# A fused two-layer decoder step: layer-norm statistics, squares and values to be split move from SBUF to PSUM

## The chip, the cores and the metric

The kernel runs on one core of one Trainium2 chip. Its time is the device time of one execution in microseconds (us), the median of several. Engines: PE is the matmul engine, DVE is VectorE, ACT is ScalarE, POOL is GpSimd, and SP issues most DMAs. Each has a queue of its own and works it off in order; semaphores hold an instruction until what it reads is written and the buffer that it writes is free. SBUF is the large on-chip memory. PSUM is the small one that PE writes its sums to: here eight banks of 512 numbers per partition, four with the tag `mm` and four with `tr`.

## The reference

Two layers run over 512 prompt tokens and 8 x 8 sample tokens with the same weights (576 columns in all). Each norm closes a residual step, and the values that follow feed the next projection:

```
h    = x * (1 + scale1) + shift1
proj = h @ w_in            # retention, sliding-window attention -> mix
x    = LN1(alpha * x + gate1 * (mix @ w_out))
h2   = x * (1 + scale2) + shift2
u    = causal depthwise conv3(h2 @ w_up);  f = (silu(u_a) * u_b) @ w_down
x    = LN2(alpha * x + gate2 * f)

mu  = mean(x);  var = mean((x - mu)^2)
LN  = (x - mu) * rsqrt(var + eps) * g + b
```

Outputs are the last `x` and the states of both groups.

## The kernel before

**Layout.** Features lie on partitions, tokens in columns: `X[0..7]` are eight tiles of 128 x 576. Work goes in two halves of 288 columns (`HA`); the second half holds 224 prompt columns and the 64 of the samples, whose gate, scale and shift differ per group of 8. That is why the second half needs small extra operations of 64 columns (L558, L560).

**Matmuls.** Products need nearly full float32. Each value is split into a rounded high part (`hi`, a cast on ACT, L290) and a rest (`lo`, a subtraction, L291), each weight likewise (`wh`, a cast on ACT, L91, and `wl`, a subtraction on POOL or DVE, L96). Every product is three matmuls: hi with wh, lo with wh, hi with wl (`gemm`). A projection of one half is 8 x 3 = 24 matmuls of 128x288. `Weights` loads weights in units of 128x1024 through two buffers `wr` (SP's queue); a load waits until the subtraction of the unit before last is done.

**The norm.** There are four: l0a and l0b after attention and after the feed-forward of layer 0, l1a and l1b in layer 1. `LayerNorm.r_done` runs as each tile `X[m]` of a half is ready: its square (ACT, L527) is added to `sq` (DVE, L528), the value to `sd` (POOL, or DVE for the last tile, L525). `stats` sums both over the partitions with a matmul by ones (`pd`, `pq`, in `tr` banks), squares the mean, subtracts it (L540), takes the root (ACT, L541) and the reciprocal (DVE, L542), and copies the mean to SBUF (ACT, L543). `norm` subtracts the mean (L548) and multiplies by the inverse (L549) for each k; `make_h` then forms `h` = x*scale + shift (ACT, L285), `hi` and `lo`.

**The order around it.** `halves` runs the last four output projections for half 0, then one for half 1, then statistics and norm of half 0, then the other three for half 1. `skewed` runs the next stage's first projections for half 0, with statistics and norm of half 1 after the first of them in the text, then for half 1. Each engine's order there is not written out: a scheduler of the compiler makes it from dependencies and free buffers, so a change of buffers moves instructions. The attention in between is pinned in written order.

**Names.** `l0a0...` is norm l0a, half 0, `l0a1...` half 1. `l0a1s` are squares, `l0asq` and `l0asd` the sums, `l0a0pd` and `l0a0pq` the PSUM results, `l0ars` the inverse. `l0wo` is the output projection, `l0up0h` the first up-projection of a half, `l0up4a` the first one after the skewed stage, `l0ghi` and `l0glo` the split values, `h0g` (l0b: `h0n`) the value before its split. `l1kv0h` is the first projection that follows l0b.

Of the kernel before, what the change touches and what calls it, by code (L numbers as in the profile page):

```python
# [121 lines left out]
def _body(ctx, tc, nc, a):  # L122
# [156 lines left out]
    def make_h(src, st, k, half, hi, lo, nm):  # L279

        s_t, t_t = st
        tmp = tok(f"h{nm}", HA)
# [1165 lines left out]
```

## Time and profile before

| | |
|---|---|
| median of 3 runs | 1529.6 us (1527.59 to 1530.27) |
| profiled execution | 1529.95 us, its span 1528.2 us |
| mean granted PE clock | 0.983 |
| PE busy | 1461.7 us, 96% of the span |
| DVE busy | 864.4 us, 57% |
| ACT busy | 643.0 us, 42% |
| POOL busy | 496.4 us, 32% |

A busy share is an average over the span: it says which engine is nearly always at work, not what is late in one stage. For that there are the list of waits (who was idle, and whose instruction ended the idle time), the timeline of an engine (each instruction with its start and duration), and the windows (busy time and granted clock in a stretch). [...] A timeline row with x2 or x3 is so many instructions in sequence.

### The profile page before, as it was taken

The numbers are of one execution on the slowest core, as the hardware profiler recorded it, in microseconds if no ns is written. First come the engines' busy times: TensorE is split into PE (matmuls) and PEld (weight loads), VectorE is DVE, ScalarE is ACT, GpSimd is POOL, SyncE is SP. The second block draws the span as 40 slices with busy tenths as digits, with TensorE's granted clock in tenths as the row PEclk, the third lists the DMA queues.
The fourth block names the chain that finished last, engine by engine and source line by source line (L and its number), as shares of the span: only waits on it lengthen the run. The fifth ranks groups of instructions, "written<-read, shape, count | busy, mean of one in ns | idle before, by whom it ended". The sixth has DMA issues, their size and how long they took to land.

```text
span 1528.2 us, 28103 instructions
## 1 busy us (share of the span) xinstructions
PE 1461.7 (96%) x11220; PEld 1368.5 (90%) x11220; DVE 864.4 (57%) x1659; ACT 643.0 (42%) x1295; POOL 496.4 (32%) x646
## 2 busy tenths in 40 slices
PE   6999989989999999999999999999799999999995
PEld 3878789979989998999988899889799999999994
DVE  3366356776644254545675664677775435544567
ACT  2335233347542144325446443333675325524543
POOL 2131212454421132223462322225543213312353
PEclk8999999999999999999999999999999999999998
DMA  9585733333364655332213333242132222223211
GB/s 347 162 284 171 244 117 105 103 104 92 101 228 157 228 167 179 93 106 83 80 56 130 118 112 97 85 113 66 56 102 85 85 84 85 83 80 93 84 49 63
DMA packets 98047, 186.37 MB, mean 122 GB/s; under 512 B 30284, under 2 KB 42620, under 8 KB 97788
## 3 DMA queue, kind: packets, MB, share of 16 engines
q1 hardware_dynamic: 82624, 176.52, 36.7%
q10 hardware_dynamic: 15292, 8.06, 1.8%
q8 instruction: 88, 1.44, 0.4%
q14 instruction: 43, 0.35, 0.1%
HBM read 169.56 MB, written 11.83 MB: 119 GB/s over the span
## 4 chain that ended last, share of the span: by engine, by line
PE 81%; DVE 11%; DMA 3%; ACT 2%; issue 1%; POOL 1%; SPq 0%; ACTq 0%; POOLq 0%; DVEq 0%
PE ada L135 3%; PE l0wo L135 1%; PE l1wo L135 1%; DVE l1x L548 1%; PE l0wdl L135 1%; PE l1wdl L135 1%; DMA wr<-in_wst 1%; DVE l0x L548 1%; DVE l1x L549 1%; DVE l0x L549 1%; DVE wl L96 1%; ACT l1p L663 1%; PE l1o L135 1%; PE l0o L135 1%; ACT wh L91 1%
## 5 line engine op out<-in xcount | busy, mean ns | idle before, releaser
L91 ACT CAST wh<-wr 128x1024 fp32r<-128x1024 f32 x192 | 200.5, 1047 | 316.1 <-PE l0rv2b L135 11.9
L96 POOL TENSOR_TENSOR wl<-wr,wh 128x1024 fp32r<-128x1024 f32 x65 | 158.1, 2432 | 399.1 <-ACT wh L91 349.2
L96 DVE TENSOR_TENSOR wl<-wr,wh 128x1024 fp32r<-128x1024 f32 x127 | 161.2, 1270 | 165.0 <-ACT wh L91 146.1
L1160 POOL COPY l0edge<-l0u 128x2 f32<-128x2 f32 x44 | 38.3, 871 | 134.1 <-ACT l0u L1154 134.1
L1160 POOL COPY l1edge<-l1u 128x2 f32<-128x2 f32 x44 | 38.3, 871 | 120.6 <-ACT l1u L1154 120.6
L1168 DVE SCALAR_TENSOR_TENSOR l0c<-l0u,par,l0c 128x592 f32<-128x592 f32 x44 | 48.3, 1100 | 49.3 <-ACT l0c L1167 46.7
L1168 DVE SCALAR_TENSOR_TENSOR l1c<-l1u,par,l1c 128x592 f32<-128x592 f32 x44 | 48.6, 1106 | 46.3 <-ACT l1c L1167 43.6
L135 PE MATMUL ada<-wa,cs 128*32 128x512 f32 (+1 forms) x416 | 59.2, 584 | 5.2 <-DVE cs L185 5.1
L135 PEld LDWEIGHTS ada<-wa,cs 128*32 128x32 f32 x416 | 15.0, 112 | 32.5 <-issue 17.5
L1167 ACT ACTIVATE l0c<-l0u,par 128x592 f32<-128x592 f32 x44 | 38.8, 884 | 3.6 <-ACT l0u L1155 0.4
L1167 ACT ACTIVATE l1c<-l1u,par 128x592 f32<-128x592 f32 x44 | 38.8, 884 | 3.3
L1169 DVE SCALAR_TENSOR_TENSOR l1c<-l1u,par,l1c 128x592 f32<-128x592 f32 x44 | 36.6, 834 | 1.4
L1169 DVE SCALAR_TENSOR_TENSOR l0c<-l0u,par,l0c 128x592 f32<-128x592 f32 x44 | 36.6, 834 | 1.4
L479 ACT CAST l0fhi<-l0c 128x512 fp32r<-128x512 f32 (+1 forms) x44 | 16.8, 430 | 46.5 <-DVE l0c L1174 46.5
L479 ACT CAST l1fhi<-l1c 128x512 fp32r<-128x512 f32 (+1 forms) x44 | 16.9, 431 | 37.8 <-DVE l1c L1174 37.8
L792 POOL TENSOR_TENSOR l1sw<-l1sw,c_sin 128x576 f32<-128x576 f32 x8 | 14.9, 1857 | 50.6 <-DMA l1sw<-l1raw 47.9
L792 POOL TENSOR_TENSOR l0sw<-l0sw,c_sin 128x576 f32<-128x576 f32 x8 | 13.6, 1697 | 43.9 <-DMA l0sw<-l0raw 43.9
L480 DVE TENSOR_TENSOR l1flo<-l1c,l1fhi 128x512 fp32r<-128x512 f32 (+1 forms) x44 | 18.2, 455 | 13.0 <-ACT l1fhi L479 13.0
L480 DVE TENSOR_TENSOR l0flo<-l0c,l0fhi 128x512 fp32r<-128x512 f32 (+1 forms) x44 | 18.2, 455 | 12.4 <-ACT l0fhi L479 12.4
L1173 ACT ACTIVATE l1c<-l1c 128x592 f32<-128x592 f32 x22 | 15.4, 698 | 15.2 <-DVE l1c L1169 15.2
L235 DVE TENSOR_TENSOR mod<-adat,par 128x36 f32<-128x36 f32 (+1 forms) x26 | 3.7, 185 | 31.6 <-PE adat L138 31.6
L1173 ACT ACTIVATE l0c<-l0c 128x592 f32<-128x592 f32 x22 | 15.3, 698 | 13.6 <-DVE l0c L1169 13.6
(3182 smaller groups left out, 5936.0 us busy)
## 6 DMA issues: line engine op xcount, KB each, us to landing
wr<-in_wst SPq DMA_DIRECT2D x192, 512.0 KB, 3.6
wa<-in_w_ada SPq DMA_DIRECT2D x192, 256.0 KB, 4.9
x<-in_xT SPq DMA_DIRECT2D x8, 288.0 KB, 6.2
l0sw<-l0raw SPq DMA_DIRECT2D x32, 72.0 KB, 2.0
l0xb<-in_xT SPq DMA_DIRECT2D x8, 288.0 KB, 3.3
x_spill<-l0x ACTq DMA_DIRECT2D x8, 288.0 KB, 3.2
l1sw<-l1raw SPq DMA_DIRECT2D x32, 72.0 KB, 2.1
l1xb<-x_spill SPq DMA_DIRECT2D x8, 288.0 KB, 3.1
```

The costliest lines, as they stand in the source:

```text
L91: cast = nc.scalar.copy(hi, raw)
L96: sub = eng.tensor_tensor(lo, raw, hi.bitcast(F32), ALU.subtract)
L135: self._add(nc.tensor.matmul(*args, **kw))
L479: S.copy(hi, src)
L480: V.tensor_tensor(lo, src, hi.bitcast(F32), ALU.subtract)
L548: eng.tensor_tensor(x[:, o], x[:, o], self.sd[:, o], ALU.subtract)
L549: (eng if both else V).tensor_tensor(x[:, o], x[:, o], self.rs[:, o], ALU.mult)
L1160: G.tensor_copy(cm[:, 0:2], t[:, 512:514])
L1167: S.activation(c, t[:, 0:592], AF.Identity, bias=w[3], scale=w[0])
L1168: V.scalar_tensor_tensor(c, t[:, 1:593], w[1], c, ALU.mult, ALU.add)
L1169: V.scalar_tensor_tensor(c, t[:, 2:594], w[2], c, ALU.mult, ALU.add)
L1173: S.activation(ca, ca, AF.Silu)
```

## The change

Six edits go together. `SKEW_TAGS` gives all skewed projections `mm` banks; before, every third one took a `tr` bank. The square `t` goes to a `tr` bank, and becomes the first operand of the add. In the three norms that are not the last, the reciprocal overwrites the bank `pq`, and the mean is read from the bank `pd`, without its copy. All subtractions of the mean and all `lo` are DVE's (before, `SUB_POOL` and `LO_POOL` gave POOL two or three subtractions and two `lo` of each half). The value `h` before its split lies in a `tr` bank. The last norm (`tail`) keeps its inverse and mean in SBUF and its share for POOL.

```
--- before.py
+++ after.py
@@ -30,12 +30,10 @@
 N_IN, N_OUT, N_UP, N_DN = 22, 8, 44, 22
 UNITS = N_IN + N_OUT + N_UP + N_DN
 MM = 4
-SKEW_TAGS = ("mm", "mm", "tr")
+SKEW_TAGS = ("mm",)
 SKEW_OUT = 4
 SKEW_DN = 4
 SKEW_END = 4
-SUB_POOL = ((6, 7), (5, 6, 7))
-LO_POOL = ((1, 3), (1, 3))
 Y_POOL = ((2, 4, 6), (2, 4, 6))
 Y_DVE = ((1, 5), (5, 7))
 HEADS = (slice(0, 64), slice(64, 128))
@@ -279,7 +277,7 @@
     def make_h(src, st, k, half, hi, lo, nm):
 
         s_t, t_t = st
-        tmp = tok(f"h{nm}", HA)
+        tmp = psum("tr", f"h{nm}")
         o = half * HA
         n = HA if half == 0 else NP - HA
         S.activation(tmp[:, 0:n], src[:, o:o + n], AF.Identity, bias=t_t[:, k, 0:1], scale=s_t[:, k, 0:1])
@@ -288,7 +286,7 @@
             V.tensor_tensor(tv, src[:, NP:NT].rearrange("p (b t) -> p b t", b=8), bc(s_t[:, k, 1:9], 2, 8), ALU.mult)
             V.tensor_tensor(tv, tv, bc(t_t[:, k, 1:9], 2, 8), ALU.add)
         S.copy(hi[:, o:o + HA], tmp[:, 0:HA])
-        (G if k in LO_POOL[half] else V).tensor_tensor(lo[:, o:o + HA], tmp[:, 0:HA], hi[:, o:o + HA].bitcast(F32), ALU.subtract)
+        V.tensor_tensor(lo[:, o:o + HA], tmp[:, 0:HA], hi[:, o:o + HA].bitcast(F32), ALU.subtract)
 
     scr = dp.tile([P, 8, 384], F32, name="bias_rows", tag="bias_rows")
     scr1 = dp.tile([8, 384], F32, name="bias_row", tag="bias_row")
@@ -487,12 +485,13 @@
     junk = cp.tile([P, 1], F32, name="junk", tag="junk")
 
     class LayerNorm:
-        def __init__(self, X, nm):
-            self.X, self.nm = X, nm
+        def __init__(self, X, nm, tail=False):
+
+            self.X, self.nm, self.tail, self.mean, self.inv = X, nm, tail, {}, {}
             self.shift = unit("S", f"{nm}sh")
             self.sd = unit("S", f"{nm}sd")
             self.sq = unit("S", f"{nm}sq")
-            self.rs = unit("S", f"{nm}rs")
+            self.rs = unit("S", f"{nm}rs") if tail else None
 
         def shift_base(self, m, half, base):
 
@@ -523,9 +522,9 @@
                 G.tensor_tensor(self.sd[:, o], self.X[0][:, o], x[:, o], ALU.add)
             else:
                 (V if m == 7 else G).tensor_tensor(self.sd[:, o], self.sd[:, o], x[:, o], ALU.add)
-            t = tok(f"{nm}s{m}", HA)
+            t = psum("tr", f"{nm}s{m}")[:, 0:HA]
             S.activation(t, x[:, o], AF.Square)
-            V.tensor_tensor(self.sq[:, o], self.sq[:, o], t, ALU.add)
+            V.tensor_tensor(self.sq[:, o], t, self.sq[:, o], ALU.add)
 
         def stats(self, half, tail=False):
             o, nm = slice(half * HA, half * HA + HA), f"{self.nm}{half}"
@@ -539,14 +538,19 @@
             S.activation(t, pd[:, 0:HA], AF.Square)
             V.tensor_tensor(t, pq[:, 0:HA], t, ALU.subtract)
             S.activation(t, t, AF.Sqrt, bias=eps_ln)
-            V.reciprocal(self.rs[:, o], t)
-            S.copy(self.sd[:, o], pd[:, 0:HA])
-
-        def norm(self, k, half, eng=V, both=False):
+            if self.tail:
+                V.reciprocal(self.rs[:, o], t)
+                S.copy(self.sd[:, o], pd[:, 0:HA])
+                self.mean[half], self.inv[half] = self.sd[:, o], self.rs[:, o]
+            else:
+                V.reciprocal(pq[:, 0:HA], t)
+                self.mean[half], self.inv[half] = pd[:, 0:HA], pq[:, 0:HA]
+
+        def norm(self, k, half, eng=V):
             o = slice(half * HA, half * HA + HA)
             x = self.X[k]
-            eng.tensor_tensor(x[:, o], x[:, o], self.sd[:, o], ALU.subtract)
-            (eng if both else V).tensor_tensor(x[:, o], x[:, o], self.rs[:, o], ALU.mult)
+            eng.tensor_tensor(x[:, o], x[:, o], self.mean[half], ALU.subtract)
+            eng.tensor_tensor(x[:, o], x[:, o], self.inv[half], ALU.mult)
 
     def add_gated(ps, half, g, m, base, out, nm):
 
@@ -1115,7 +1119,7 @@
 
         def norm_h(half, st, nm):
             for k in range(KT):
-                ln.norm(k, half, G if k in SUB_POOL[half] else V)
+                ln.norm(k, half)
                 make_h(X[k], st, k, half, h[k][0], h[k][1], f"{l}{nm}{k}{half}")
 
         def out_half(m, half):
@@ -1240,7 +1244,7 @@
             if lastg:
                 while side:
                     tick()
-                ln = LayerNorm(X, f"{L}b")
+                ln = LayerNorm(X, f"{L}b", l + 1 == DEPTH)
             full = KT - (SKEW_END if l + 1 == DEPTH else SKEW_DN) if lastg else KT
             for m in range(full):
                 tick()
@@ -1268,7 +1272,7 @@
         def y_out(half):
             o = slice(half * HA, half * HA + HA)
             for k in range(KT):
-                ln.norm(k, half, G if k in Y_POOL[half] else V, True)
+                ln.norm(k, half, G if k in Y_POOL[half] else V)
                 if k % 2 == 0:
                     y = tok(f"y{k}{half}", 2 * HA)
                 y_k = y[:, k % 2 * HA:k % 2 * HA + HA]
```

DVE at the statistics of half 0 in l0a, before: the last square's add of this stretch, the variance (L540), the reciprocal, and between and behind them subtractions (L548) and multiplications (L549).

```order
L528 TENSOR_TENSOR l0asq<-l0asq,l0a1s_3582 128x288
L540 TENSOR_TENSOR l0a0var<-l0a0pq,l0a0var 128x288
L548 TENSOR_TENSOR l0x_3080<-l0x_3080,l0asd 128x288
L548 TENSOR_TENSOR l0x_3154<-l0x_3154,l0asd 128x288
L542 RECIPROCAL l0ars<-l0a0var 128x288
L548 TENSOR_TENSOR l0x_3228<-l0x_3228,l0asd 128x288
L549 TENSOR_TENSOR l0x_3080<-l0x_3080,l0ars 128x288
L549 TENSOR_TENSOR l0x_3154<-l0x_3154,l0ars 128x288
L549 TENSOR_TENSOR l0x_3228<-l0x_3228,l0ars 128x288
```

The same place now (L527 is the add, L539 the variance, L546 the reciprocal, L552 the subtraction, L553 the multiplication).

```order
L527 TENSOR_TENSOR l0asq<-l0a1s_3581,l0asq 128x288
L552 TENSOR_TENSOR l0x_3079<-l0x_3079,l0a0pd 128x288
L539 TENSOR_TENSOR l0a0var<-l0a0pq,l0a0var 128x288
L552 TENSOR_TENSOR l0x_3153<-l0x_3153,l0a0pd 128x288
L552 TENSOR_TENSOR l0x_3227<-l0x_3227,l0a0pd 128x288
L546 RECIPROCAL l0a0pq<-l0a0var 128x288
L552 TENSOR_TENSOR l0x_3301<-l0x_3301,l0a0pd 128x288
L553 TENSOR_TENSOR l0x_3079<-l0x_3079,l0a0pq 128x288
L553 TENSOR_TENSOR l0x_3153<-l0x_3153,l0a0pq 128x288
```

The order of steps is nearly the same, but no row has two SBUF tiles as inputs any more, and one more subtraction stands ahead of the first multiplication.

ACT from the root of the same statistics on, before: one weight cast (`wh`, unit 31), then values `h` (L285) and casts to `hi` (L290).

```order
L541 ACTIVATE l0a0var<-l0a0var,eps_ln 128x288
L91 CAST wh_3518<-wr_3516 128x1024
L285 ACTIVATE h0g_3597<-l0x_3080,st_0t,st_0s 128x288
L285 ACTIVATE h0g_3603<-l0x_3154,st_0t,st_0s 128x288
L290 CAST l0ghi_3374<-h0g_3597 128x288
L285 ACTIVATE h0g_3609<-l0x_3228,st_0t,st_0s 128x288
L290 CAST l0ghi_3376<-h0g_3603 128x288
L285 ACTIVATE h0g_3615<-l0x_3302,st_0t,st_0s 128x288
L290 CAST l0ghi_3378<-h0g_3609 128x288
```

The same now (L89 is a weight cast, L283 the value, L288 the cast to `hi`).

```order
L540 ACTIVATE l0a0var<-l0a0var,eps_ln 128x288
L89 CAST wh_3517<-wr_3515 128x1024
L283 ACTIVATE h0g_3595<-l0x_3079,st_0t,st_0s 128x288
L283 ACTIVATE h0g_3601<-l0x_3153,st_0t,st_0s 128x288
L288 CAST l0ghi_3373<-h0g_3595 128x288
L89 CAST wh_3750<-wr_3748 128x1024
L288 CAST l0ghi_3375<-h0g_3601 128x288
L283 ACTIVATE h0g_3607<-l0x_3227,st_0t,st_0s 128x288
L288 CAST l0ghi_3377<-h0g_3607 128x288
L283 ACTIVATE h0g_3613<-l0x_3301,st_0t,st_0s 128x288
L89 CAST wh_3860<-wr_3858 128x1024
L288 CAST l0ghi_3379<-h0g_3613 128x288
```

The casts of units 32 and 33, which stood behind the eighth `hi`, now stand ahead of the second and the fourth.

POOL in the same stretch, before: weight subtractions (L96) of units 30 and 31, the running sum (L525), two subtractions of the mean (L548) and two `lo` (L291).

```order
L96 TENSOR_TENSOR wl_3479<-wr_3476,wh_3478 128x1024
L525 TENSOR_TENSOR l0asd<-l0asd,l0x_3392 128x288
L548 TENSOR_TENSOR l0x_3473<-l0x_3473,l0asd 128x288
L548 TENSOR_TENSOR l0x_3513<-l0x_3513,l0asd 128x288
L96 TENSOR_TENSOR wl_3519<-wr_3516,wh_3518 128x1024
L291 TENSOR_TENSOR l0glo_3377<-h0g_3603,l0ghi_3376 128x288
L291 TENSOR_TENSOR l0glo_3381<-h0g_3615,l0ghi_3380 128x288
L525 TENSOR_TENSOR l0asd<-l0asd,l0x_3433 128x288
L525 TENSOR_TENSOR l0asd<-l0asd,l0x_3473 128x288
```

And now (L94 is the weight subtraction, of units 30 to 33; L524 the running sum).

```order
L94 TENSOR_TENSOR wl_3478<-wr_3475,wh_3477 128x1024
L524 TENSOR_TENSOR l0asd<-l0asd,l0x_3391 128x288
L1148 MEMSET l0u_3780 128x2
L1149 COPY l0u_3780<-l0edge_3778 128x8x2
L94 TENSOR_TENSOR wl_3518<-wr_3515,wh_3517 128x1024
L94 TENSOR_TENSOR wl_3751<-wr_3748,wh_3750 128x1024
L94 TENSOR_TENSOR wl_3861<-wr_3858,wh_3860 128x1024
L524 TENSOR_TENSOR l0asd<-l0asd,l0x_3432 128x288
L524 TENSOR_TENSOR l0asd<-l0asd,l0x_3472 128x288
```

The mean's subtractions and the `lo` are gone from POOL; units 32 and 33 follow unit 31 at once, and x5 and x6 of the running sum come behind them.

## Rows read from the trace of the kernel before

**Rows 1.** Page, part 4: the chain that ended last, share of the span by engine.

```profile
PE 81%; DVE 11%; DMA 3%; ACT 2%; issue 1%; POOL 1%; SPq 0%; ACTq 0%; POOLq 0%; DVEq 0%
```

**Rows 2.** Waits of PE, 300 to 372 us: engine, waited for; total, times, longest us.

```profile
PE l0a1pd L135 <- DVE l0asd L525: 4.0, 1, 4.0
PE l0up0h L135 <- POOL l0glo L291: 2.2, 1, 2.2
PE l0up0h L135 <- DVE l0glo L291: 1.6, 2, 1.3
PE l0up0h L135 <- ACT l0ghi L290: 1.2, 2, 0.7
```

**Rows 3.** Timeline of PE in l0a: start, duration, what [idle before, releaser].

```profile
330.33 0.30 PE L135 MATMUL l0wo<-l0mrlo,wh 128*128 128x288 f32 x1
330.47 0.29 PE L135 MATMUL l0wo<-l0mrhi,wl 128*128 128x288 f32 x1
...
344.60 0.85 PE L135 MATMUL l0a1pd<-l0asd,ones_f 128*128 128x288 f32 x1 [3.98 <-DVE l0asd L525]
...
370.36 0.29 PE L135 MATMUL l0up4a<-l0ghi,wh 128*128 128x288 f32 x1
```

**Rows 4.** Windows: stretch, length; busy (x) of PE, PEld, DVE, ACT, POOL; PEclk; DMA.

```profile
344.60:350.00 5.40, 5.40 (x18) 4.83 (x19) 2.65 (x6) 1.24 (x3) 2.86 (x3) 0.50 0.64 210
350.00:352.00 2.00, 2.00 (x17) 2.00 (x16) 2.00 (x2) 0.00 (x0) 0.00 (x0) 0.97 0.05 19
```

**Rows 5.** Timeline of DVE in l0a.

```profile
321.65 2.33 DVE L528 TENSOR_TENSOR l0asq<-l0asq,l0a1s 128x288 f32<-128x288 f32 x1 [0.57 <-ACT l0a1s L527]
323.90 0.45 DVE L540 TENSOR_TENSOR l0a0var<-l0a0pq,l0a0var 128x288 f32<-128x288 f32 x1
...
325.86 1.94 DVE L542 RECIPROCAL l0ars<-l0a0var 128x288 f32<-128x288 f32 x1
327.73 1.56 DVE L548 TENSOR_TENSOR l0x<-l0x,l0asd 128x288 f32<-128x288 f32 x1
...
331.05 0.45 DVE L549 TENSOR_TENSOR l0x<-l0x,l0ars 128x288 f32<-128x288 f32 x1
...
339.24 2.63 DVE L528 TENSOR_TENSOR l0asq<-l0asq,l0a1s 128x288 f32<-128x288 f32 x1
...
342.11 2.43 DVE L525 TENSOR_TENSOR l0asd<-l0asd,l0x 128x288 f32<-128x288 f32 x1
```

**Rows 6.** Timeline of POOL in l0a.

```profile
321.27 2.39 POOL L96 TENSOR_TENSOR wl<-wr,wh 128x1024 fp32r<-128x1024 f32 x1 [5.92 <-ACT wh L91]
323.62 1.03 POOL L525 TENSOR_TENSOR l0asd<-l0asd,l0x 128x288 f32<-128x288 f32 x1
...
326.58 2.39 POOL L96 TENSOR_TENSOR wl<-wr,wh 128x1024 fp32r<-128x1024 f32 x1
...
339.02 2.54 POOL L96 TENSOR_TENSOR wl<-wr,wh 128x1024 fp32r<-128x1024 f32 x1 [0.89 <-ACT wh L91]
...
341.89 2.34 POOL L96 TENSOR_TENSOR wl<-wr,wh 128x1024 fp32r<-128x1024 f32 x1
```

**Rows 7.** Timeline of ACT in l0a.

```profile
329.75 1.15 ACT L285 ACTIVATE h0g<-l0x,st_0t,st_0s 128x288 f32<-128x288 f32 x2 [3.89 <-DVE l0x L549]
```

**Rows 8.** Timeline of SP's queue in l0a, then the page's part 6 (DMA issues).

```profile
329.00 0.33 SPq L82 DMA_DIRECT2D wr<-in_wst  x1
...
wr<-in_wst SPq DMA_DIRECT2D x192, 512.0 KB, 3.6
```

**Rows 9.** Groups by line and form, DVE: busy, mean ns | idle before.

```profile
L890 DVE SCALAR_TENSOR_TENSOR l1sn<-l1s,c_gch,l1dls 128x512 f32<-128x512 f32 x4 | 3.0, 745 | 1.9 <-PE l1dls L135 1.9
...
L957 DVE SCALAR_TENSOR_TENSOR l0gT<-l0oT,l0gT 128x512 f32<-128x512 f32 x4 | 2.8, 692 | 4.3 <-PE l0oT L138 4.3
```

**Rows 10.** Waits of PE, 1040 to 1112 us, then 770 to 830 us.

```profile
PE l1a1pd L135 <- DVE l1asd L525: 4.0, 1, 4.0
...
PE l1kv0h L135 <- POOL l0nlo L291: 2.2, 1, 2.2
```

More of the change, by code (lines that the diff above doesn't have):

```diff
@@ L32 @@
 MM = 4
-SKEW_TAGS = ("mm", "mm", "tr")
+SKEW_TAGS = ("mm",)
 SKEW_OUT = 4
@@ L36 @@
 SKEW_END = 4
-SUB_POOL = ((6, 7), (5, 6, 7))
-LO_POOL = ((1, 3), (1, 3))
 Y_POOL = ((2, 4, 6), (2, 4, 6))
@@ L281, in make_h @@
         s_t, t_t = st
-        tmp = tok(f"h{nm}", HA)
+        tmp = psum("tr", f"h{nm}")
         o = half * HA
@@ L290, in make_h @@
         S.copy(hi[:, o:o + HA], tmp[:, 0:HA])
-        (G if k in LO_POOL[half] else V).tensor_tensor(lo[:, o:o + HA], tmp[:, 0:HA], hi[:, o:o + HA].bitcast(F32), ALU.subtract)
+        V.tensor_tensor(lo[:, o:o + HA], tmp[:, 0:HA], hi[:, o:o + HA].bitcast(F32), ALU.subtract)
     scr = dp.tile([P, 8, 384], F32, name="bias_rows", tag="bias_rows")
@@ L489, in _body, with __init__ @@
     class LayerNorm:
-        def __init__(self, X, nm):
-            self.X, self.nm = X, nm
+        def __init__(self, X, nm, tail=False):
+            self.X, self.nm, self.tail, self.mean, self.inv = X, nm, tail, {}, {}
             self.shift = unit("S", f"{nm}sh")
@@ L494, in __init__ @@
             self.sq = unit("S", f"{nm}sq")
-            self.rs = unit("S", f"{nm}rs")
+            self.rs = unit("S", f"{nm}rs") if tail else None
         def shift_base(self, m, half, base):
@@ L525, in r_done @@
                 (V if m == 7 else G).tensor_tensor(self.sd[:, o], self.sd[:, o], x[:, o], ALU.add)
-            t = tok(f"{nm}s{m}", HA)
+            t = psum("tr", f"{nm}s{m}")[:, 0:HA]
             S.activation(t, x[:, o], AF.Square)
-            V.tensor_tensor(self.sq[:, o], self.sq[:, o], t, ALU.add)
+            V.tensor_tensor(self.sq[:, o], t, self.sq[:, o], ALU.add)
         def stats(self, half, tail=False):
@@ L541, in stats, with norm @@
             S.activation(t, t, AF.Sqrt, bias=eps_ln)
-            V.reciprocal(self.rs[:, o], t)
-            S.copy(self.sd[:, o], pd[:, 0:HA])
-        def norm(self, k, half, eng=V, both=False):
+            if self.tail:
+                V.reciprocal(self.rs[:, o], t)
+                S.copy(self.sd[:, o], pd[:, 0:HA])
+                self.mean[half], self.inv[half] = self.sd[:, o], self.rs[:, o]
+            else:
+                V.reciprocal(pq[:, 0:HA], t)
+                self.mean[half], self.inv[half] = pd[:, 0:HA], pq[:, 0:HA]
+        def norm(self, k, half, eng=V):
             o = slice(half * HA, half * HA + HA)
             x = self.X[k]
-            eng.tensor_tensor(x[:, o], x[:, o], self.sd[:, o], ALU.subtract)
-            (eng if both else V).tensor_tensor(x[:, o], x[:, o], self.rs[:, o], ALU.mult)
+            eng.tensor_tensor(x[:, o], x[:, o], self.mean[half], ALU.subtract)
+            eng.tensor_tensor(x[:, o], x[:, o], self.inv[half], ALU.mult)
     def add_gated(ps, half, g, m, base, out, nm):
@@ L1117, in norm_h @@
             for k in range(KT):
-                ln.norm(k, half, G if k in SUB_POOL[half] else V)
+                ln.norm(k, half)
                 make_h(X[k], st, k, half, h[k][0], h[k][1], f"{l}{nm}{k}{half}")
@@ L1242, in _body @@
                     tick()
-                ln = LayerNorm(X, f"{L}b")
+                ln = LayerNorm(X, f"{L}b", l + 1 == DEPTH)
             full = KT - (SKEW_END if l + 1 == DEPTH else SKEW_DN) if lastg else KT
@@ L1270, in y_out @@
             for k in range(KT):
-                ln.norm(k, half, G if k in Y_POOL[half] else V, True)
+                ln.norm(k, half, G if k in Y_POOL[half] else V)
                 if k % 2 == 0:
```

## The prediction

> **What bounds the kernel now.** I read the chain that ended last first: the matmul engine (PE) holds 81% of it and VectorE (DVE) 11% [rows 1]. So time is to be had where PE waits, or where it runs at the lower clock, and nowhere else. The list of PE's waits, taken over the first norm of layer 0 (l0a, 300 to 372 us), is second: 4.0 us for the running sum of the values (`asd`), 2.2 for a low half (`lo`) that POOL makes, 1.6 and 1.2 for low and high halves of DVE and ACT, together 9.0 [rows 2]. Third, PE's own rows: the last `wo` matmul starts at 330.47, the sums at 344.60, and `up4a`, the first after the stage, at 370.36 [rows 3]. Between lie 192 projection matmuls (four of 8 x 3 for each half), 0.13 apart at full clock (330.33 to 330.47 [rows 3]; I take 0.132), so 25.3 us, and the four sum matmuls, about 1. From 330.60 the stage would end at 356.9. It ends 13.5 later. [...]
>
> Fourth, DVE's rows show why the data are late. A 128x288 operation takes 0.45 us (next one 0.37 after it) when alone, but the add of a square takes 2.33 at 321.65 and 2.63 at 339.24, the add of the last value 2.43 at 342.11 [rows 5]. Each stands beside one of POOL's weight subtractions (`wl`, 2.39 from 321.27, 2.54 from 339.02, 2.34 from 341.89 [rows 6]). All stretched ones read two SBUF tiles. The variance (L540) at 323.90 has one operand in PSUM and takes 0.45 beside a POOL row that runs from 323.62 to 324.65 [rows 5, 6].
>
> **The change, part by part, in l0a.**
> *The add of the square.* With the square in PSUM it has one SBUF operand. At 321.65 it should take 0.45 instead of 2.33: 1.9 us. Behind it the variance, its root and the reciprocal (1.94 [rows 5]) follow; the subtractions of the mean that DVE fits between, one of them at 1.56 [rows 5], go to 0.45. The root keeps its turn on ACT. I walk DVE's new order: add to 322.1, variance about 322.9, root 323.1 to 323.7, reciprocal 323.8 to 325.7, one subtraction, first multiplication done at 326.5. Today ACT waits until 329.75 for that multiplication [rows 7], so the lead is 3.2 us. PE can use little of it by itself, since it is busy with `wo` until 330.60.
>
> *The low halves.* All eight are DVE's. PE waits 2.2 for one of POOL's [rows 2]; that wait goes. DVE gains two subtractions and two low halves per half (three subtractions in the other), at 0.37 each: 1.5 to 1.9. What DVE loses by stretch (1.9 at the first square, 2.2 at a later one, 2.0 at the value, 1.1 at a subtraction [rows 5]) is more.
>
> *What takes the place of the waits.* `h` now lies in one of four `tr` banks; mean and inverse hold two until the last subtraction and multiplication. So a third `h` waits for the first `lo`, the fourth for the second, the fifth for the third, the sixth for DVE's last subtraction. Where ACT ran from `h` to `hi` without a stop, it now hands over to DVE and back for each pair. Also the weight casts of units 32 and 33 now stand among the eight `hi`: unit 33's ahead of the fourth. Its load is issued when POOL has finished unit 31's subtraction: 329.00 today [rows 8], right behind 326.58 + 2.39 [rows 6]. Without the two subtractions that POOL does from 324.65 on, ahead of it [rows 6], that ends at about 327.2; loads take 3.6 [rows 8], I take 4.0 for the crowd here, so the cast runs from 331.2 to 332.2, and the fourth `hi` ends at 332.7. Laying PE's new order on this, I get five waits, 0.98, 0.35, 0.66, 0.33 and 0.14: 2.45 in place of 5.0 for `lo` and `hi`. Saved: 2.6. Were every hand-over free it would be 5.0, and if the load came as late as now (3.9 us wait of ACT [rows 7]) about 0.
>
> *The sums.* The square of x7 and the value's sum are no longer stretched, and POOL does unit 33's subtraction about six microseconds sooner, so x7's add to `asd` (three SBUF operands still) no longer meets it. I have `asd` at 338.65 and `asq` at 339.25, and the two sum matmuls stand at the end of `up1`, 14 matmuls later in PE's order: due at 339.25. The 4.0 goes whole. Bounds: 4.0, or about 2 if one more stretched add remains ahead of it.
>
> *The clock.* With no idle of microseconds in one piece I expect no fall: of 5.4 us at 0.50 the same matmuls need about half. Saved 2.6, bounds 0 and 2.7. This hangs on the former two.
>
> *The other half.* Its eight `h` go through the same two banks while `up0` to `up3` eat them. DVE's work there is 24 x 0.37 + 16 small ones x 0.13 = 11.0 against 96 x 0.132 = 12.7 of matmuls, so it is hidden but for the start: I count 0.6 of new waits.
>
> Sum in l0a: 2.6 + 4.0 + 2.6 - 0.6 = 8.6.
>
> *The price of a PSUM operand.* The nearest rows: an operation with its first operand in SBUF and the second in PSUM takes 0.745 for 128x512, one with the first in PSUM 0.692 [rows 9]: 0.053 more. Sixteen subtractions and multiplications per half have that shape: 0.85, exposed in the first half at most. The eight low halves, with the first operand in PSUM, cost nothing more. Bounds 0 and 0.85 per norm; I take 0, since PE's five waits hang on ACT and banks, and keep the end for the range. [...]
>
> **The other norms.** l1a repeats l0a, with the same 4.0 as its longest wait [rows 10]: 8.6 again. At l0b no wait is that long; the longest is 2.2, for POOL's low half [rows 10]. There the cast of unit 99 stands ahead of the third `hi`, its load is issued when POOL's unit 97 is done, and I have ACT held until about 796, a wait of 2.1 in place of the 2.2 that goes. The reciprocal starts no sooner, since that root stood behind another cast. I take 2.0, about one such wait and no more, bounds 0 and 4.0 (both go). The last norm, l1b, keeps its mean and inverse in SBUF and its POOL share; only the squares move: one DVE operation less ahead of the last value, 0.3.
>
> Sum: 8.6 + 8.6 + 2.0 + 0.3 = 19.5. The profiled execution took 1529.95, its span 1528.2; the median of three is 1529.6. 1529.95 - 19.5 = 1510.45, less the 0.35 by which this execution lay above the median: 1510.1, say 1510.
>
> **Rivals.**
> *The waits move to ACT and the banks.* The cast of unit 33 lands 2 us or more later than worked out, or each hand-over costs twice what I took. Then PE idles 5 us again in the first half, in a long enough piece that the clock goes to 0.50 as it did after the 4.0. Only that 4.0 is saved, less 0.6: 3.4 in each of l0a and l1a, 0 in l0b: 1523. For it: loads of 3.6 us against a margin of nothing. Against: POOL's two subtractions ahead of that load are gone.
>
> *The change doesn't do what it says.* If adds with a PSUM operand are still stretched, DVE has only more work: 6.6 from POOL's low halves (3 x 2.2) against 3 x 1.9 of moved operations: 0.9 gained, 1528.7. Against: L540 beside POOL at 0.45.
>
> *DVE becomes the bound (slower).* Price s on each of the 24 operations per half, from their PSUM operand. The first half is exposed by 24s, the second by 24s less its slack of 1.7 (12.7 - 11.0). Three norms: 3 x (48s - 1.7) against 19.5, so it decides from s = 0.17. Were such an operation to take twice its 0.37, the time would be 48 longer than forecast, some 1558. The rows show 0.05 at most [rows 9], but none has DVE write PSUM and ACT read it back at this pace, in order, through two banks.
>
> [...]
>
> **How the numbers follow.** The forecast (1503 to 1517) 0.68; the waits at ACT 0.15; no effect 0.07; DVE or the banks as bound 0.10. The low end is 1510 less 2 x 2.4 (hand-overs free) and 2 in l0b: 1503. The high end takes the second case in, with a little behind it: 1524. A measurement of this kernel tells about 0.2%, 3 us. Faster by more: 0.68 + 0.15 = 0.83; within: 0.07; slower: 0.10. The likeliest is 1510.
>
> **What would show it.** Right: the wait of `l0a1pd` and `l1a1pd` gone, or under 0.5; the granted clock 0.9 or more through the stage; adds of squares at 0.45 beside `wl`; `up4a`, now 39.9 us after the last `wo` matmul of l0a, about 31 after it; five short PE waits on `hi` and `lo` in the first half. Wrong: one PE wait of 2 us or more on a `hi` behind the cast of unit 33 or 99; subtractions and multiplications above 0.6; a clock of 0.50 left in l0a.

## The result

The changed kernel takes 1509.45 us (median of 4 runs, 1506.47 to 1513.48), the kernel before 1528.96 in the same comparison. The ratio is 0.9874, with a 95% interval of 0.9846 to 0.9902: 1.3% faster. Forecast was 1510. Of all the runs below, one execution (of the kernel with the squares in SBUF) took 4938 us, over three times the others, and is left out of that kernel's median.

The profiled execution has a span of 1509.6 us, 18.6 less than the one before. The table cuts every span at the same instructions of PE: a norm stage runs from its first mean matmul (`l0a0mean` and so on) to the first matmul behind the stage (`up4a`, or `l1r01a` after l0b); l1b runs to the end. Starts are those of PE's timeline, in us; differences were taken before rounding.

| | before | changed | difference |
|---|---|---|---|
| ahead of l0a | 284.3 | 283.3 | -1.1 |
| l0a | 86.0 | 77.0 | -9.0 |
| feed-forward 0 | 383.3 | 383.2 | 0.0 |
| l0b | 75.4 | 73.6 | -1.8 |
| attention 1 | 194.8 | 197.6 | +2.8 |
| l1a | 86.0 | 77.0 | -9.0 |
| feed-forward 1 | 357.4 | 357.4 | 0.0 |
| l1b to the end | 61.0 | 60.5 | -0.5 |

The four stages with a norm give 20.3. The attention of layer 1, which the change does not touch, gives 2.8 back in this execution (the last section says more of that).

### The profile page after: what moved, and what is told of

It is laid out like the page before. It is cut to its first block, busy times and chain, and to the rows that moved or that the text cites. A ratio compares the mean times of both kernels' runs of the same rounds, so it can differ in the third digit from the quotient of the medians.

```text
span 1509.6 us, 28060 instructions
## 1 busy us (share of the span) xinstructions
PE 1460.4 (97%) x11220; PEld 1369.7 (91%) x11220; DVE 840.1 (56%) x1686; ACT 638.9 (42%) x1289; POOL 458.7 (30%) x619
## 4 chain that ended last, share of the span: by engine, by line
PE 87%; DVE 4%; DMA 4%; ACT 2%; POOL 1%; issue 1%; SPq 0%; ACTq 0%; DVEq 0%; POOLq 0%
PE ada L133 3%; DMA wr<-in_wst 2%; PE l1wo L133 1%; PE l0wo L133 1%; PE l0wdl L133 1%; PE l1wdl L133 1%; ACT wh L89 1%; POOL wl L94 1%; PE l0o L133 1%; PE l1o L133 1%; DMA bias_rows<-bias_row 1%; PE l0kv L133 1%; ACT l1p L667 0%; PE l0up1h L133 0%; PE l1up1h L133 0%
## 5 line engine op out<-in xcount | busy, mean ns | idle before, releaser
L89 ACT CAST wh<-wr 128x1024 fp32r<-128x1024 f32 x192 | 201.0, 1047 | 328.1 <-DMA wr<-in_wst 24.2
L94 POOL TENSOR_TENSOR wl<-wr,wh 128x1024 fp32r<-128x1024 f32 x65 | 157.1, 2417 | 430.4 <-ACT wh L89 364.1
L94 DVE TENSOR_TENSOR wl<-wr,wh 128x1024 fp32r<-128x1024 f32 x127 | 159.5, 1256 | 168.2 <-ACT wh L89 149.1
L1172 DVE SCALAR_TENSOR_TENSOR l0c<-l0u,par,l0c 128x592 f32<-128x592 f32 x44 | 46.7, 1065 | 45.0 <-ACT l0c L1171 42.3
L478 DVE TENSOR_TENSOR l0flo<-l0c,l0fhi 128x512 fp32r<-128x512 f32 (+1 forms) x44 | 18.1, 453 | 11.7 <-ACT l0fhi L477 11.7
L795 DVE TENSOR_TENSOR l1raw<-l1raw,c_cos 128x576 f32<-128x576 f32 x8 | 11.1, 1387 | 20.3 <-DMA l1sw<-l1raw 16.1
```

Of the source, the lines that this page charges most:

```text
L89: cast = nc.scalar.copy(hi, raw)
L94: sub = eng.tensor_tensor(lo, raw, hi.bitcast(F32), ALU.subtract)
L478: V.tensor_tensor(lo, src, hi.bitcast(F32), ALU.subtract)
L795: V.tensor_tensor(raw, raw, cos_t, ALU.mult)
L1172: V.scalar_tensor_tensor(c, t[:, 1:593], w[1], c, ALU.mult, ALU.add)
```

## The profile after

The chain that ended last, by engine, now holds hardly any DVE:

```profile
PE 87%; DVE 4%; DMA 4%; ACT 2%; POOL 1%; issue 1%; SPq 0%; ACTq 0%; DVEq 0%; POOLq 0%
```

It was PE 81% and DVE 11% [rows 1]. The waits of PE in the l0a, l0b and l1a stages (total, times, longest; line numbers of the changed kernel are a few off those of before) answer to [rows 2, 10]:

```profile
PE l0up0h L133 <- ACT l0ghi L288: 1.1, 2, 0.8
...
PE l1kv0h L133 <- ACT l0nhi L288: 3.0, 4, 1.6
...
PE l1up0h L133 <- ACT l1ghi L288: 1.2, 2, 0.9
```

The 4.0 us for the sums and the 2.2 us for POOL's low half are gone in l0a and l1a; what is left is ACT's high half. At l0b there is 3.0 of it. PE's timeline in l0a shows where they lie:

```profile
329.42 0.29 PE L133 MATMUL l0wo<-l0mrhi,wl 128*128 128x288 f32 x1
329.55 0.29 PE L133 MATMUL l0up0h<-l0ghi,wh 128*128 128x288 f32 x1
...
331.67 0.40 PE L133 MATMUL l0up0h<-l0ghi,wh 128*128 128x288 f32 x1 [0.76 <-ACT l0ghi L288]
...
333.01 0.40 PE L133 MATMUL l0up0h<-l0ghi,wh 128*128 128x288 f32 x1 [0.32 <-ACT l0ghi L288]
...
339.69 0.65 PE L133 MATMUL l0a1pd<-l0asd,ones_f 128*128 128x288 f32 x2
...
360.31 0.29 PE L133 MATMUL l0up4a<-l0ghi,wh 128*128 128x288 f32 x1
```

The next stage's first matmul follows the last `wo` matmul by 0.13 us, so the first value is there in time. Two waits stand ahead of the fourth and the fifth high half, and none at the sums (339.69). `up4a` comes 30.9 us after the last `wo` matmul, where it was 39.9 [rows 3]. DVE's rows of the same stretch:

```profile
320.51 0.46 DVE L527 TENSOR_TENSOR l0asq<-l0a1s,l0asq 128x288 f32<-128x288 f32 x1 [0.48 <-ACT l0a1s L526]
...
322.64 1.95 DVE L546 RECIPROCAL l0a0pq<-l0a0var 128x288 f32<-128x288 f32 x1
...
331.65 0.46 DVE L289 TENSOR_TENSOR l0glo<-h0g,l0ghi 128x288 fp32r<-128x288 f32 x1 [1.12 <-ACT l0ghi L288]
...
337.12 0.46 DVE L524 TENSOR_TENSOR l0asd<-l0asd,l0x 128x288 f32<-128x288 f32 x1
339.11 0.46 DVE L527 TENSOR_TENSOR l0asq<-l0a1s,l0asq 128x288 f32<-128x288 f32 x1 [1.53 <-ACT l0a1s L526]
```

The adds of squares (L527) and of the last value (L524) take 0.46 us, where single ones took 2.33, 2.63 and 2.43 [rows 5]. The first add and the low half at 331.65 lie beside two of these weight subtractions of POOL:

```profile
320.18 2.40 POOL L94 TENSOR_TENSOR wl<-wr,wh 128x1024 fp32r<-128x1024 f32 x1 [5.89 <-ACT wh L89]
...
327.80 2.41 POOL L94 TENSOR_TENSOR wl<-wr,wh 128x1024 fp32r<-128x1024 f32 x1 [1.00 <-ACT wh L89]
331.39 2.36 POOL L94 TENSOR_TENSOR wl<-wr,wh 128x1024 fp32r<-128x1024 f32 x1 [1.19 <-ACT wh L89]
```

The last weight subtraction of this stretch ends at 333.75. The last two adds (337.12 and 339.11) come after it, so their 0.46 does not show what an operand in PSUM does; the first of them still has all its operands in SBUF.

ACT shows what holds the fourth high half: unit 33's cast (L89), which waits 0.82 us for its load and then takes 1.05, stands ahead of it.

```profile
325.34 1.11 ACT L283 ACTIVATE h0g<-l0x,st_0t,st_0s 128x288 f32<-128x288 f32 x2 [1.02 <-DVE l0x L553]
...
330.27 1.05 ACT L89 CAST wh<-wr 128x1024 fp32r<-128x1024 f32 x1 [0.82 <-DMA wr<-in_wst]
```

And the windows of PE (columns as in [rows 4]; PEclk is the granted clock as a share of full speed) show that the clock still falls, to 0.63 and 0.51, now behind the two waits on high halves (before, behind the 4.0 us for the sums [rows 4]) and for a shorter time than the 5.4 us of before:

```profile
334.00:336.00 2.00, 2.00 (x12) 2.00 (x12) 1.94 (x8) 1.25 (x5) 0.80 (x1) 0.63 0.42 111
336.00:338.00 2.00, 2.00 (x11) 2.00 (x10) 1.47 (x5) 0.39 (x1) 1.55 (x7) 0.51 0.86 328
338.00:340.00 2.00, 2.00 (x16) 1.95 (x16) 0.46 (x1) 0.72 (x2) 0.00 (x0) 1.00 0.47 131
```

## The experiments

Theory A: DVE operations with two SBUF inputs are stretched when they lie beside POOL's weight subtractions; an operand in PSUM frees them, and the waits of PE were the outcome. Rival B: the gain is the work taken from POOL, or the new banks and the order that the scheduler makes of them. Stage lengths are as in the table above; the norm stages of the two kernels add up to 308.4 and 288.1 us. Two executions of one order (the changed kernel and its control below) differ by under 0.3 us in a norm stage, save where the clock falls in one and not in the other.

**The squares alone.** On the kernel before:

```
-            t = tok(f"{nm}s{m}", HA)
+            t = psum("tr", f"{nm}s{m}")[:, 0:HA]
...
-            V.tensor_tensor(self.sq[:, o], self.sq[:, o], t, ALU.add)
+            V.tensor_tensor(self.sq[:, o], t, self.sq[:, o], ALU.add)
```

> The kernel before, with the squares alone in PSUM. Theory A (DVE operations with two SBUF inputs are stretched beside POOL's weight subtractions, and an operand in PSUM frees them): the adds of squares go from 2.3 and 2.6 us to 0.45, but the value's add beside the last weight subtraction, POOL's low halves and the subtractions of the mean stay. The wait of the sums falls from 4.0 to about 2 in l0a and l1a, some of the clock comes back: 1521 to 1525 us. Rival B (the gain is that of work taken from POOL, or of banks and order): no gain, 1528 to 1530.

1525.67 us, ratio 0.9975 (0.9963 to 0.9986); stages 301.1 us, 7.3 less. DVE in l0a, with POOL's weight subtractions from 322.56, 327.85 and 339.95:

```profile
322.90 0.46 DVE L528 TENSOR_TENSOR l0asq<-l0a1s,l0asq 128x288 f32<-128x288 f32 x1 [0.48 <-ACT l0a1s L527]
...
328.03 2.52 DVE L548 TENSOR_TENSOR l0x<-l0x,l0asd 128x288 f32<-128x288 f32 x1
...
340.00 2.62 DVE L291 TENSOR_TENSOR l0glo<-h0g,l0ghi 128x288 fp32r<-128x288 f32 x1
```

The add is short beside a weight subtraction, as theory A has it; but a subtraction of the mean and a low half, both with SBUF inputs, now fall beside the next two and take 2.5 and 2.6. The stretch moves to whatever stands there. Of PE's waits in l0a the longest in total is now the one for DVE's low halves; the wait for the sums, which I expected at about 2, is not in the list of l0a, and in l1a it is 0.5:

```profile
PE l0up0h L135 <- DVE l0glo L291: 3.7, 5, 2.0
```

```profile
PE l1a1pd L135 <- DVE l1asd L525: 0.5, 1, 0.5
```

The gain in the median is 4 us, a little less than expected, and less than the 7.3 of the stages: in the profiled execution, one of the two slowest of the twelve, the attention of layer 1, which this edit does not touch, took 199.7 us (194.8 before).

**POOL's share to DVE alone.** On the kernel before:

```
-SUB_POOL = ((6, 7), (5, 6, 7))
-LO_POOL = ((1, 3), (1, 3))
+SUB_POOL = ((), ())
+LO_POOL = ((), ())
```

> The kernel before, with POOL's subtractions of the mean and low halves given to DVE, all operands in SBUF as before. Theory A: POOL's low half no longer holds PE (2.2 in three norms), but DVE has 4 to 5 more operations per half that are stretched beside weight subtractions; 1525 to 1534 us. Rival B (taking the work from POOL is the gain): 1511 to 1516.

1516.39 us, ratio 0.9909 (0.9892 to 0.9925); stages 296.7, 11.7 less. This is at the rival's number, and faster than I expected of theory A. More than half of the gain comes without any operand in PSUM: the low half of POOL for which PE waited 2.2 us [rows 2] is no longer POOL's. That POOL also reaches the weight subtractions sooner is my reading of its order. What stays stretched is there too (weight subtractions from 317.17, 330.07 and 336.50):

```profile
317.55 2.33 DVE L528 TENSOR_TENSOR l0asq<-l0asq,l0a1s 128x288 f32<-128x288 f32 x1 [0.57 <-ACT l0a1s L527]
...
330.73 2.25 DVE L291 TENSOR_TENSOR l0glo<-h0g,l0ghi 128x288 fp32r<-128x288 f32 x1
...
336.78 2.64 DVE L528 TENSOR_TENSOR l0asq<-l0asq,l0a1s 128x288 f32<-128x288 f32 x1
```

**Mean and inverse in SBUF.** On the changed kernel, the last norm's branch for all four:

```
-            if self.tail:
+            if True:
                 V.reciprocal(self.rs[:, o], t)
                 S.copy(self.sd[:, o], pd[:, 0:HA])
```

> The changed kernel, with mean and inverse copied to SBUF in all four norms as in the last; squares and values to be split stay in PSUM, all subtractions and multiplications stay on DVE. Theory A: these 16 operations per half have two SBUF inputs again, and POOL's weight subtractions lie beside nearly all of half 0 in l0a and l1a; single ones take 1.5 to 2.3 us; PE waits 4 us or more in the first half, clock at 0.50 for longer: 1520 to 1530 us. Rival B: 1508 to 1512, or faster, since two banks come free earlier for the values.

1519.13 us, ratio 0.9931 (0.9916 to 0.9946); stages 299.0, 10.9 more than the changed kernel. DVE in l0a (two weight subtractions take 4.95 from 333.98), then the waits of PE:

```profile
334.61 4.64 DVE L553 TENSOR_TENSOR l0x<-l0x,l0ars 128x288 f32<-128x288 f32 x2
```

```profile
PE l0up1h L133 <- DVE gs_0a L562: 3.5, 1, 3.5
```

Two multiplications take 4.64 us in place of 0.8; behind them PE waits 3.5 for the bank that the next evacuation frees. That is theory A's mechanism (with 1.0 for high halves the waits in l0a make 4.5); its range from 1520 us on was a little too high.

**The value in SBUF.** On the changed kernel:

```
-        tmp = psum("tr", f"h{nm}")
+        tmp = tok(f"h{nm}", HA)
```

> The changed kernel, with the value before its split back in SBUF (so ten buffers and no hand-over through two banks). Theory A: the low halves have two SBUF inputs; about four of eight in the first half of l0a and l1a lie beside weight subtractions and take up to 2 us more: 1514 to 1522 us. Rival (the two banks cost more than the stretch): 1504 to 1508.

1521.39 us, ratio 0.995 (0.9932 to 0.9968); stages 300.7, 12.5 more, with 7.1 of it in l0a and as much in l1a. One low half, and a small add of 64 columns, lie beside weight subtractions (330.97 and 336.63):

```profile
331.25 2.39 DVE L289 TENSOR_TENSOR l0glo<-h0g,l0ghi 128x288 fp32r<-128x288 f32 x1
...
337.28 2.03 DVE L564 TENSOR_TENSOR l0x<-gs_0a,l0xb 128x64 f32<-128x64 f32 x1
```

PE waits 1.8 us for that low half and 0.8 for the sums of half 1. That is not all of the 7.1: at the start of half 1 PE waits 2.6 more in three pieces for high halves of ACT, with no weight subtraction on POOL beside them, and the clock falls again behind these: the matmuls of 128x288 start 0.24 us apart from 356.3 to 359.0.

```profile
355.49 0.40 PE L133 MATMUL l0up0h<-l0ghi,wh 128*128 128x288 f32 x1 [1.20 <-ACT l0ghi L288]
```

The order of PE is another here: `up0` of half 1 goes alone until 356.6, where the changed kernel takes `up0` to `up3` of half 1 by turns. How much of the 12.5 is stretch and how much is order was not separated. In l0b this kernel is 1.3 us faster than the changed one (72.2 against 73.6), and PE waits 1.1 for high halves there in place of 3.0: in that norm the hand-over through two banks, my rival here, costs more than the stretch.

**Squares in SBUF.** On the changed kernel; the trace is that of a single further execution.

```
-            t = psum("tr", f"{nm}s{m}")[:, 0:HA]
+            t = tok(f"{nm}s{m}", HA)
...
-            V.tensor_tensor(self.sq[:, o], t, self.sq[:, o], ALU.add)
+            V.tensor_tensor(self.sq[:, o], self.sq[:, o], t, ALU.add)
```

> The changed kernel, with the squares back in SBUF and the sum as first operand. Theory A: the add ahead of the variance lies beside unit 30's weight subtraction and takes about 2.3 us again; the reciprocal and all behind it come 2 us later, of which PE's lead (3 us before it needs the first value) hides most. l0a from the last wo matmul to up4a 31 to 33.5 us (30.9 in the changed kernel, 39.9 before); 1510 to 1516 us. Rival B: 30.9 and 1509.

> The same kernel as squares_sbuf, for its trace. Theory A: the add ahead of the variance 2.3 us beside unit 30's weight subtraction, stage l0a 78 to 80 us (77.0 in the changed kernel). Rival B: 0.45 and 77.0.

1511.79 us (median of four), ratio 0.9902 (0.9872 to 0.9931), an interval that overlaps that of the changed kernel; the further execution 1511.38. The add is stretched, as expected:

```profile
322.22 2.33 DVE L527 TENSOR_TENSOR l0asq<-l0asq,l0a1s 128x288 f32<-128x288 f32 x1 [0.57 <-ACT l0a1s L526]
```

but l0a is 77.3 (77.0; I had expected 78 to 80), the stages 289.2 (288.1), and PE's wait for the sums only this:

```profile
PE l0a1pd L133 <- DVE l0asd L524: 0.4, 1, 0.4
```

So once the rest is there, the squares are worth 1 us in the stages: most of the lead that they give is not used, and the weight subtraction that had met the last adds ends at 336.7, before them, for other reasons. The clock hides a part: in this execution it stays at 1.00 through l0a and l1a, while it falls in both in the changed kernel (0.51 from 336 to 338 us, 0.50 from 1065 to 1067). Against a stage of the changed kernel's order without a fall (75.6, in the control below) the squares are worth 1.7 in l1a.

**The tags.** Undone in the changed kernel (this diff), and done alone in the kernel before (its reverse):

```
-SKEW_TAGS = ("mm",)
+SKEW_TAGS = ("mm", "mm", "tr")
```

> The changed kernel, with every third skewed projection in a tr bank, as before. Two banks are left for values to be split, minus the one that a projection holds for up to 24 matmuls; in l0a unit 33's cast stands behind all eight high halves. If banks are what makes the hand-over work: l0a 33 to 38 us, 1514 to 1522. If the cast ahead of the fourth high half is what is left of the waits: l0a 29 to 30.5, 1504 to 1508.

> The kernel before, with the tags of the skewed projections alone changed. If tags are needed only because values to be split now take tr banks: no gain, 1526 to 1531 us, stage l0a 85 to 88. If the other order of PE (up0 finished first, sums later) is itself a gain: 1518 to 1524, l0a 82 to 84.

Undone: 1529.49 us, ratio 1.001 (0.9998 to 1.0023): the whole gain is lost (stages 311.0, 22.9 more), more than either of my numbers. The third projection of half 0, the one with a `tr` bank, no longer stands between the sums and the first value of half 1 (it is evacuated at 362.6 us), so it does not fill PE there; that the values to be split take its bank is my reading of the order. PE's timeline in l0a, then windows:

```profile
347.51 0.29 PE L133 MATMUL l0up3h<-l0ghi,wl 128*128 128x288 f32 x1
351.63 0.61 PE L133 MATMUL l0up0h<-l0ghi,wh 128*128 128x288 f32 x1 [3.82 <-ACT l0ghi L288]
```

```profile
348.00:350.00 2.00, 0.00 (x0) 0.00 (x0) 2.00 (x5) 0.75 (x3) 0.00 (x0) 0.98 0.02 8
352.00:354.00 2.00, 2.00 (x9) 1.94 (x9) 2.00 (x9) 1.88 (x5) 0.00 (x0) 0.50 0.01 4
```

PE waits 3.82 us, and behind it the clock is 0.50 from 352 to 354 us. In the changed kernel two projections (48 matmuls at 0.132, 6.3 us) stand in that place. This is not only a matter of l0a and l1a: l0b takes 80.8 us (73.6), with 5.8 of waits on high halves. Done alone: 1532.56 us, ratio 1.0022 (1.0011 to 1.0034), slower by 0.2%, with the old waits in place:

```profile
PE l0a1pd L135 <- DVE l0asd L525: 3.3, 1, 3.3
```

**The weight subtractions to DVE.** On the kernel with POOL's share on DVE (all in SBUF), units 30 to 33 and their like in layer 1 are DVE's as well:

```
-        early = v < 3 or N_IN + N_OUT <= v < N_IN + N_OUT + 4
+        early = v < 3
...
-        eng = nc.gpsimd if (early and u != 2) or (v % 3 == 2 and not late and u != 2) else nc.vector
+        eng = nc.gpsimd if (early and u != 2) or (v % 3 == 2 and not late and u != 2 and not N_IN + N_OUT <= v < N_IN + N_OUT + 4) else nc.vector
```

> The kernel with POOL's subtractions of the mean and low halves on DVE (all in SBUF), and also the weight subtractions of the four units of the norm after attention on DVE. Theory A: with no weight subtraction on POOL beside them, all adds, subtractions, multiplications and low halves of l0a and l1a take 0.37 to 0.46 us, though all operands lie in SBUF; DVE has four times 1.2 us more. l0a 33 to 37 us (35.4 without this edit), 1511 to 1519. Rival (they are stretched for another reason, as DMA traffic): single ones of 1.5 us and more stay.

1513.18 us, ratio 0.9908 (0.9881 to 0.9934); l0a 79.9 (81.6 without this edit). DVE in l0a, with no weight subtraction on POOL in the stretch:

```profile
325.60 0.45 DVE L528 TENSOR_TENSOR l0asq<-l0asq,l0a1s 128x288 f32<-128x288 f32 x1
...
330.01 0.81 DVE L549 TENSOR_TENSOR l0x<-l0x,l0ars 128x288 f32<-128x288 f32 x2
...
341.80 1.04 DVE L528 TENSOR_TENSOR l0asq<-l0asq,l0a1s 128x288 f32<-128x288 f32 x1
```

With the neighbour gone, the same operations on SBUF take 0.45, multiplications too (0.81 for two). Three are longer from 322 us on (a low half 0.70, an add of a square 1.04 and one of DVE's own weight subtractions 1.81, which take 1.2 otherwise), and each lies beside one of POOL's running sums (from 338.98, 340.75 and 323.79). This takes the suspected neighbour away and leaves the operands, as the squares alone took an operand away and left the neighbour; theory A holds for the stretch itself. The whole time gains nothing by it (0.9908 against 0.9909): the weight subtractions now delay PE themselves:

```profile
PE l0up3h L135 <- DVE wl L96: 3.1, 1, 3.1
```

**Three load buffers.** On the changed kernel, to see what the hold of ACT costs; nine token buffers make room, and a control has these alone:

```
-        self.raw[u] = self.pool.tile([P, 1024], F32, tag="wr", name=f"wr{u}", bufs=2)
+        self.raw[u] = self.pool.tile([P, 1024], F32, tag="wr", name=f"wr{u}", bufs=3)
...
-        return up.tile([P, w], F32, tag="T", name=name, bufs=10)
+        return up.tile([P, w], F32, tag="T", name=name, bufs=9)
```

> The changed kernel, with three load buffers for weights in place of two (and nine token buffers in place of ten, to make room). Unit 33's and 99's loads no longer wait for a subtraction; ACT's cast is not held. If the hold is what leaves PE 0.8 and 1.6 us idle and the clock at 0.50 behind it: l0a 28.5 to 29.5 us (30.9), l0b 30 to 32 (34.3), 1500 to 1505 us. If the two banks are: as the changed kernel, 1509, l0a 30.9.

> The changed kernel with nine token buffers in place of ten, and two load buffers as it has: the control for the run with three load buffers. If the third load buffer made that gain: stage l0a (from its first mean matmul to up4a) 77.0 us as in the changed kernel, and not 74.8. If the token buffers did: 74.8.

1501.07 us, ratio 0.9823 (0.9799 to 0.9847); stages 282.5, l0a and l1a 74.8 each. The control, one execution: 1508.9, l0a 77.1. ACT's cast is no longer held; in l0a one wait of PE is left, and the granted clock stays at 1.00 in l0a and l1a:

```profile
328.67 0.40 PE L133 MATMUL l0up0h<-l0ghi,wh 128*128 128x288 f32 x1 [0.32 <-ACT l0ghi L288]
```

```profile
325.00:339.00 14.00, 13.38 (x92) 12.25 (x91) 11.86 (x32) 8.68 (x20) 6.32 (x10) 1.00 0.56 183
1053.00:1067.00 14.00, 13.38 (x92) 12.25 (x91) 11.96 (x32) 8.60 (x20) 5.47 (x10) 1.00 0.28 80
```

l0b gains only 0.5 (73.1): there the cast itself (1.05 us from 777.56, without a wait for its load) stands ahead of the third high half, and PE waits 1.15 us for that one. I had expected 2 to 4.

**And the gated product in its bank.** On top of that:

```
-            t = small(f"gs_{nm}", 64)
-            V.tensor_tensor(t.rearrange("p (b t) -> p b t", b=8), ps[:, n:HA].rearrange("p (b t) -> p b t", b=8),
+            t = ps[:, n:HA]
+            V.tensor_tensor(t.rearrange("p (b t) -> p b t", b=8), t.rearrange("p (b t) -> p b t", b=8),
```

> Three load buffers, nine token buffers, and the gated product of the 64 sample columns written back to its PSUM bank rather than to a small SBUF tile, so that its add has one SBUF operand. Theory A: in l0b that add takes 0.2 instead of 1.64 beside a weight subtraction, and the reciprocal comes 1.4 earlier: l0b 71.5 to 72.5 us (73.1 with three buffers alone), 1498 to 1501. Rival: l0b is held by ACT's order of casts: 73.1 and 1501.

1496.50 us, ratio 0.9789 (0.9764 to 0.9814); stages 280.9. The small add of l0b, here and in the kernel without this edit:

```profile
769.83 0.23 DVE L562 TENSOR_TENSOR l0wdl<-l0wdl,g 128x64 f32<-128x64 f32 x1
770.10 0.23 DVE L564 TENSOR_TENSOR l0x<-l0wdl,l0x 128x64 f32<-128x64 f32 x1
```

```profile
768.49 1.64 DVE L564 TENSOR_TENSOR l0x<-gs_0bl,l0x 128x64 f32<-128x64 f32 x1
```

0.23 us in place of 1.64, but l0b is 72.6 (73.1): 0.5 of the 1.4. Counted from the start of the stage the reciprocal comes 0.9 earlier; that ACT's casts hide the rest is my reading of its order. It is the fastest kernel of this study; whether it beats the one with three load buffers alone stays open, since their intervals overlap (runs of 1495.5 to 1502.7 against 1498.8 to 1502.5).

## Why the prediction was right, and where its steps were not

*The sum.* l0a and l1a were to gain 8.6 each and gained 9.0; l0b 2.0 and 1.8; l1b 0.3 and 0.5. For l0b the number is partly luck: the prediction set a new wait of 2.1 against the 2.2 that goes, which nets 0.1, and took 2.0 all the same. What the traces show there is 2.2 gone for POOL's low half, 1.2 gone for the sums (a wait that the prediction did not count), and 1.3 more for ACT's high halves (3.0 against 1.7). The price of PSUM operands was taken as 0, with 0.05 as bound. In the groups of DVE by line (mean ns behind the bar and the busy time), operations with the mean or inverse in PSUM take 0.44 us, no more than the 0.45 of an SBUF one that stands alone, and the last norm's, still in SBUF and partly beside POOL's share of it, a mean of 0.91:

```profile
L552 DVE TENSOR_TENSOR l1x<-l1x,l1bsd 128x288 f32<-128x288 f32 x10 | 8.8, 910 | 0.0
...
L552 DVE TENSOR_TENSOR l0x<-l0x,l0a0pd 128x288 f32<-128x288 f32 x8 | 3.4, 445 | 0.2 <-ACT l0a0var L538 0.2
```

Of the 0.053 more for a second operand in PSUM, measured at 128x512 [rows 9], nothing shows here. The rivals with a DVE bound and with no effect are out; of the rival with waits at ACT a small part came true, the fourth high half of l0a and the third of l0b, and three load buffers took the former away.

*The walk through the new order* held to within a fraction of a microsecond. Taken from the last `wo` matmul, which came 1.05 earlier in this execution: reciprocal at 322.64 (forecast 323.8 less 1.05), ACT's first value at 325.34, where the multiplication was to be done at 326.5 less 1.05, unit 33's cast at 330.27 (331.2 less 1.05). The sum of squares of half 1 is the exception: it ends at 339.57, 1.4 later than the 339.25 less 1.05 of the forecast, and it cost nothing, since PE came to the sums at 339.69.

*"Five waits, 2.45"* was too much: the fourth is 0.76 us (0.98 forecast), the fifth 0.32, and the others do not come, nor the 0.6 of half 1. It made 2 us more than forecast.

*"With no idle of microseconds in one piece I expect no fall"* failed, and took most of these 2 us back. The clock goes to 0.50 behind waits of 0.76 and 0.32; "a clock of 0.50 left in l0a" was one of the prediction's own signs of being wrong, and it was there. What it costs the control kernel shows by itself, since in one execution it fell in l0a and not in l1a, behind the same two waits, 0.32 us being the second each time (PE's timeline of the first, then windows):

```profile
333.76 0.40 PE L133 MATMUL l0up0h<-l0ghi,wh 128*128 128x288 f32 x1 [0.88 <-ACT l0ghi L288]
...
1062.40 0.40 PE L133 MATMUL l1up0h<-l1ghi,wh 128*128 128x288 f32 x1 [0.90 <-ACT l1ghi L288]
```

```profile
334.00:341.00 7.00, 6.50 (x33) 5.86 (x33) 5.34 (x18) 4.34 (x12) 4.19 (x9) 0.76 0.62 208
1061.00:1068.00 7.00, 5.59 (x36) 4.67 (x36) 5.47 (x19) 5.88 (x14) 4.34 (x9) 1.00 0.55 151
```

l0a took 77.1 us and l1a 75.6: 1.5 for the fall. The prediction's working (at 0.50 half of the time is lost) gives 1.7 for 7 us at a mean of 0.76, near the 1.5, so its price of 2.6 for the old fall, the 5.4 us at 0.50 [rows 4], was a fair one. Half is a little much: in l0a of the changed kernel the matmuls of 128x288 start 0.24 us apart at 0.50 (335.10 to 337.50) and 0.13 apart at 1.00 (338.11 to 339.16). But the step "no long wait, no fall" is refuted; with one wait of 0.32 left (three load buffers) it did not fall in either stage. Why it fell in one stage of the control and not in the other stays open.

*Which part does it* I had wrong in two places. I laid the 4.0 us of the sums to short squares and an earlier weight subtraction together, with half of it left if one add stayed stretched. Either takes most of it away by itself: with the squares back in SBUF the wait is 0.4, with the squares alone on the kernel before it is 0.5 in l1a. And I put no price on the tags; without them nothing is left of the gain. The parts do not add up: alone on the kernel before they give 7.3 (squares), 11.7 (POOL's share) and 5.1 lost (tags) in the stages; taken singly from the changed kernel they cost 1.1 (squares), 10.9 (statistics), 12.5 (value) and 22.9 (tags). Each edit also changes the scheduler's order, so these are prices of an edit with its order, not of stretch alone. Rival B has a share that I had not given it: more than half of the gain is there with POOL's subtractions of the mean and low halves moved and all in SBUF.

*The total* came out at 1509.45 also because the untouched parts of the kernel varied by as much as my steps were off (2.8 more in the attention of layer 1, 1.1 less ahead of l0a).

## What to carry to other kernels

Look for short operations of one engine that last as long as a long one of its neighbour, as DVE's adds of 2.33 to 2.63 us did here beside POOL's weight subtractions of 2.34 to 2.54: then try to take away the neighbour, or one of the two SBUF inputs, of every operation in that stretch. With the squares alone moved, the stretch went on to the next ones that had two (2.52 and 2.62 us). When banks are given a new use, count what is left for the work that filled the gap before: here nothing of the gain is left without the tags (1529.49 us), which look like bookkeeping, and they give none by themselves (1532.56). And compare stages between fixed instructions rather than whole runs: that tells 1 us in a kernel whose executions differ by 7.

## What was not expected of the hardware

The parts that no edit touched were not equally steady. Over thirteen traces the two feed-forward parts stayed within 383.24 to 383.28 and 357.34 to 357.37 us, while the stretch ahead of l0a took 279.6 to 287.0 and the attention of layer 1 193.0 to 199.7. In the changed kernel's execution the latter held a wait of 1.4 us behind a weight subtraction of DVE that took 2.33 (from 838.95), and the granted clock was 0.50 from 844 to 848. Its control, in the same order, took 194.7: the subtraction took 2.33 there too (from 840.18), but PE waited 0.56 behind it, and the clock stayed at 1.00. So the stretch is not what differs; what is was not tried.
